# Memory values of three layers from seven block products instead of eight, in five of eight feature pairs

## The chip, the cores and the metric

The kernel runs on one core of one Trainium2 chip. The metric is the device time of one execution in microseconds, the median over the runs of a kernel.

## The reference

A decoder trunk of four layers over 256 tokens of width 2048, all in fp32. Each layer projects its tokens, mixes them in one of three ways, and also lets four memory heads attend to a fixed memory of 256 rows. The part that the change touches is the memory's own projection, which needs no token and is done for all layers before the first layer starts:

```python
mem_n = _rmsnorm(mem, mem_norm)                    # (256, 2048)
for i in range(DEPTH):                             # DEPTH = 4
    ...
    mem_out = _memory_attention(mq, mem_n @ w_mem_kv[i])   # w_mem_kv[i]: (2048, 2048)
# in _memory_attention: mk, mv = jnp.split(mem_kv, 2, axis=-1)   keys: 1024 columns, values: 1024 columns
```

So for every layer a 256 x 2048 matrix is multiplied by a 2048 x 1024 matrix for the keys (mk) and by another for the values (mv).

## The kernel before

fp32 precision is reached with two fp32r parts. Every weight tile `wr` that SyncE loads (128 x 1024, 512 KB) is split: ScalarE copies it to the high part `wh` (line 59, called from `split_in_order`), VectorE subtracts to get the low part `wl` (line 73). The activations are split in the same way once; `mT` holds the memory with features on the partitions, both parts. Each product of a weight tile with an activation tile is then three matmuls of 512 columns: high by high, high by low, low by high (lines 328 to 330 in `rows_by`). There are 5 buffers for `wr` and 3 each for `wh` and `wl`, so the splits run at most a few tiles ahead of TensorE.

`memory()` is the phase of the change. It takes eight turns (i, p_), four layers by two halves of 512 columns. In each turn `rows_by` computes the values' half (accumulator `acc_mv`) and then the keys' half (`acc_mk`), each over 16 feature tiles in steps of two: 96 matmuls, 8 weight tiles. `values` scales the values' accumulator by the row norm, splits it and stores it to DRAM; the keys' accumulator is copied by ScalarE (`mkz`), transposed in blocks by VectorE (`mkT`, line 544) and stored. A table `jobs` puts other work at the sixth feature tile and at the end of a key product: bias tables, loads of x and its first norm (`x_rows`, `x_features`, `nm.chunk`, `nm.finish`), and the eight copies of the bias tables from DRAM to DRAM (`table_copies`, 1.5 MB each, on GpSimd's queue).

The order on every engine comes from a scheduler that follows the program's order and its own estimate of times; splits and the matmuls of the change are pinned to the program's order among themselves. Each engine then runs its queue strictly in that order: an instruction that waits holds up all that stand behind it on that engine. SyncE's queue of loads is such a queue as well.

```python
    def split_in_order(hi, lo, src):
        with ExitStack() as held:
            for ins in behind:
                held.enter_context(tc.issue_after(ins))
            one = copy_act(hi, src)
            two = nc.vector.tensor_sub(lo, src, f32(hi))
        behind[:] = [one.ins, two.ins]
```

Of the kernel before, what the change touches and what calls it, by code (L numbers as in the profile page):

```python
# [8 lines left out]
F32 = mybir.dt.float32  # L9
F32R = mybir.dt.float32r  # L10
# [5 lines left out]
P = 128  # L16
S = 256
# [7 lines left out]
MEMW = 1024  # L25
# [2 lines left out]
PQ, AUX, WR = 5, 4, 5  # L28
IDLE = 9
CAUSAL = [(0, 0), (0, 1), (1, 1)]  # L30


@with_exitstack
def kernel(ctx: ExitStack, tc: tile.TileContext, a: dict, out: bass.AP,
# [20 lines left out]
    def f32(ap):  # L55
        return ap.bitcast(F32)
# [384 lines left out]
    def memory():  # L441
# [44 lines left out]
        def values(i, p_, acc):  # L486
# [6 lines left out]
            for z in range(2):  # L493
                nc.gpsimd.dma_start(mv[i][p_][:, z], v[z])

        def x_features(c):
# [4 lines left out]
        jobs = [[] for _ in range(15)]  # L501
        for at, job in ((0, bias_tables), (0, lambda: x_rows(0)),
                        (1, lambda: x_rows(1)), (2, lambda: x_features(0)), (3, lambda: nm.chunk(0)),
                        (5, lambda: nm.chunk(1)), (6, lambda: x_features(2)), (9, lambda: nm.chunk(2)),
                        (11, lambda: nm.chunk(3)), (12, nm.finish)):
            jobs[at].append(job)
        for n_, at in enumerate((3, 5, 7, 8, 10, 11, 12, 13)):
            jobs[at].append(lambda n_=n_: table_copies(n_ // 4, n_ % 4))
        for i in range(depth):
            w = a["w_mem_kv"][i]  # L510
            for p_ in range(2):
                start = i == p_ == 0
                acc = rows_by(mT, 16, w, 0, (MEMW + p_ * 512, 512), "mv",
                              {s: [lambda s=s: first(s), lambda k, s=s: early(s + k)]
                               for s in range(0, 16, 2)} if start else {},
                              (lambda k, n: loaded(k // 4, k % 4, k % 4 + n) if k else None) if start else None)
                if start:
                    held.append(acc)
                else:
                    values(i, p_, acc)  # L520
                def job():
                    for f in jobs.pop(0):
                        f()
                acc = rows_by(mT, 16, w, 0, (p_ * 512, 512), "mk",
                              {k: [lambda k=k: second(k)] for k in range(0, 14, 2)} if start else {6: [job]})
                T = act.tile([P, 2, 512], F32, name="mkT", tag="pq", bufs=PQ)
                for t in range(2):
                    rows_ = wk.tile([P, 512], F32, name="mkz", tag="z", bufs=2)
                    copy_act(rows_, acc[:, t], scale=m16[:, t:t + 1])
                    turned(T[:, t], rows_, 4)  # L530
# [8 lines left out]
                job()  # L539
        assert not jobs  # L540


    def turned(T, rows_, n):
# [895 lines left out]
```

## Time and profile before

| | us |
|---|---|
| median of 2 runs (2487.89 to 2489.42) | 2488.65 |
| the profiled execution | 2491.03 |
| its span in the profile | 2489.3 |
| TensorE busy | 2474.2 |
| VectorE busy | 1773.7 |
| ScalarE busy | 1401.6 |

The profiled execution is 2.38 us above the median, and 1.73 us of it lie outside the span. Matmuls are pipelined: a matmul of 512 columns is shown with 0.39 us, but the next one starts some 0.23 us after it, so time on TensorE is read from starts. Times inside the profile are counted from the span's start.

### The profile page before, as it was taken

The page shows a single profiled execution, that of the slowest core. Times are in us where ns is not written, and L with a number is a line of the kernel's source. Part 1 is how long each engine was busy: PE and PEld are TensorE (multiplying, and loading weights), DVE is VectorE, ACT ScalarE, POOL GpSimd, SP SyncE. Part 2 cuts the span into 40 slices and gives each one's busy share as a digit, 9 for nine tenths or more (in the row PEclk, how much of TensorE's full clock was granted, in tenths as well). Part 3 has the DMA queues.
Part 4 walks back from the last instruction along what each step waited for, and adds up shares of the span by engine and source line. Part 5 has one row for each costly group of instructions (what it writes and reads, how often), then busy time and mean ns, then how long its engine had stood idle before and what let it go on. Part 6 is the DMA issues. An engine that isn't in the chain of part 4 may idle for free.

```text
span 2489.3 us, 36041 instructions
## 1 busy us (share of the span) xinstructions
PE 2474.2 (99%) x12356; PEld 2084.8 (84%) x12356; DVE 1773.7 (71%) x3025; ACT 1401.6 (56%) x2250; POOL 397.7 (16%) x635
## 2 busy tenths in 40 slices
PE   9999999999999999999999999999999999999998
PEld 7888888888888888887778888878888888888887
DVE  6555655777677676877788776877777677767677
ACT  6444545555555456655566554665665655545554
POOL 1101011211120110012222101212220111012110
PEclk9999999999999999999999999999999999999999
DMA  9888887977877768589999697999978797788874
GB/s 313 279 289 287 285 277 219 259 211 217 220 225 223 220 219 244 190 265 271 258 281 271 201 289 217 288 268 267 271 229 249 231 253 217 199 221 244 242 209 147
DMA packets 462279, 607.57 MB, mean 244 GB/s; under 512 B 79536, under 2 KB 278976, under 8 KB 460944
## 3 DMA queue, kind: packets, MB, share of 16 engines
q1 hardware_dynamic: 420704, 476.92, 64.4%
q0 software_dynamic: 40672, 127.43, 17.2%
q8 instruction: 97, 1.59, 0.3%
q10 hardware_dynamic: 720, 0.93, 0.1%
q14 instruction: 86, 0.70, 0.1%
HBM read 541.49 MB, written 76.25 MB: 248 GB/s over the span
## 4 chain that ended last, share of the span: by engine, by line
PE 96%; DVE 2%; DMA 1%; issue 0%; ACT 0%; SPq 0%; POOL 0%; DVEq 0%; ACTq 0%
PE acc_gr L329 5%; PE acc_gr L328 5%; PE acc_gr L330 5%; PE acc_mq L352 4%; PE acc_g L352 4%; PE acc_wo L328 4%; PE acc_wo L330 4%; PE acc_wo L329 4%; PE acc_qn L352 4%; PE acc_wo L241 3%; PE acc_wo L242 3%; PE acc_wo L243 3%; PE acc_q L329 2%; PE acc_mv L329 2%; PE acc_q L330 2%; PE acc_q L328 2%
## 5 line engine op out<-in xcount | busy, mean ns | idle before, releaser
L73 DVE TENSOR_TENSOR wl<-wr,wh 128x1024 fp32r<-128x1024 f32 (+2 forms) x860 | 1028.2, 1197 | 548.8 <-ACT wh L59 540.2
L59 ACT ACTIVATE wh<-wr 128x1024 fp32r<-128x1024 f32 (+2 forms) x860 | 891.9, 1038 | 814.7 <-PE acc_wo L330 100.6
L329 PE MATMUL acc_gr<-wl,xT 128*128 128x512 f32 x512 | 200.1, 391 | 0.0
L330 PE MATMUL acc_gr<-wh,xT 128*128 128x512 f32 x512 | 199.7, 390 | 0.0
L328 PE MATMUL acc_gr<-wh,xT 128*128 128x512 f32 x512 | 199.7, 390 | 0.0
L328 PE MATMUL acc_wo<-wh,y 128*128 128x512 f32 x432 | 168.5, 390 | 1.9 <-ACT wh L59 1.2
L330 PE MATMUL acc_wo<-wh,y 128*128 128x512 f32 x432 | 168.3, 390 | 0.0
L329 PE MATMUL acc_wo<-wl,y 128*128 128x512 f32 x432 | 168.3, 390 | 0.0
L352 PE MATMUL acc_g<-xT,wh 128*128 128x512 f32 x512 | 161.8, 396 | 0.0
L664 POOL DMA_DIRECT2D pL<-turn x192 | 120.6, 634 | 217.8 <-issue 76.3
L352 PE MATMUL acc_mq<-xT,wh 128*128 128x512 f32 x480 | 151.8, 396 | 0.0
L242 PE MATMUL acc_wo<-wl,y 128*128 128x512 f32 x320 | 124.9, 390 | 0.0
L241 PE MATMUL acc_wo<-wh,y 128*128 128x512 f32 x320 | 124.9, 390 | 0.0
L243 PE MATMUL acc_wo<-wh,y 128*128 128x512 f32 x320 | 124.7, 390 | 0.0
L1336 DVE TENSOR_TENSOR x<-x,acc_wo 128x1024 f32<-128x1024 f32 x92 | 111.5, 1212 | 13.5 <-PE acc_wo L330 9.5
L352 PE MATMUL acc_qn<-cT,wh 128*128 128x512 f32 x384 | 120.5, 396 | 0.0
L354 PEld LDWEIGHTS acc_g<-xT,wl 128*128 128x128 f32 x512 | 95.7, 188 | 22.4 <-DVE z L589 0.8
L329 PEld LDWEIGHTS acc_gr<-wl,xT 128*128 128x128 f32 x512 | 96.1, 188 | 21.1 <-issue 1.9
L328 PEld LDWEIGHTS acc_gr<-wh,xT 128*128 128x128 f32 x512 | 96.2, 188 | 19.4 <-ACT wh L59 0.4
L330 PEld LDWEIGHTS acc_gr<-wh,xT 128*128 128x128 f32 x512 | 96.2, 188 | 19.3
L659 POOL DMA_DIRECT2D turn<-T x56 | 42.9, 766 | 408.0 <-DVE T L653 207.4
L354 PEld LDWEIGHTS acc_mq<-xT,wl 128*128 128x128 f32 x480 | 89.0, 188 | 19.5
(370 smaller groups left out, 5608.4 us busy)
## 6 DMA issues: line engine op xcount, KB each, us to landing
wr<-in_w_out_dram SPq DMA_DIRECT2D x192, 512.0 KB, 4.7
wr<-in_w_in_a_dram SPq DMA_DIRECT2D x176, 512.0 KB, 4.9
wr<-in_w_mem_kv_dram SPq DMA_DIRECT2D x126, 512.0 KB, 6.2
wr<-in_w_in_b_dram SPq DMA_DIRECT2D x116, 512.0 KB, 5.0
wr<-in_w_in_c_dram SPq DMA_DIRECT2D x104, 512.0 KB, 5.3
wr<-in_w_uq_dram SPq DMA_DIRECT2D x192, 128.0 KB, 3.6
turn<-T POOLq DMA_DIRECT2D x40, 384.0 KB, 5.8
tab<-flat POOLq DMA_DIRECT2D x8, 1536.0 KB, 11.8
```

The costliest lines, as they stand in the source:

```text
L59: return nc.scalar.activation(o, i, AF.Copy, scale=scale)
L73: two = nc.vector.tensor_sub(lo, src, f32(hi))
L241: nc.tensor.matmul(accs[c][:, t], xh, wh[:, at], start=first, stop=False)
L242: nc.tensor.matmul(accs[c][:, t], xh, wl[:, at], start=False, stop=False)
L243: nc.tensor.matmul(accs[c][:, t], xl, wh[:, at], start=False, stop=last)
L328: nc.tensor.matmul(acc[:, t, :n], xh, wh[:, at], start=first, stop=False)
L329: nc.tensor.matmul(acc[:, t, :n], xh, wl[:, at], start=False, stop=False)
L330: nc.tensor.matmul(acc[:, t, :n], xl, wh[:, at], start=False, stop=last)
L352: nc.tensor.matmul(acc[j], wh[:, at[j]], q[:, :, kt % 4, :], start=first, stop=False)
L354: nc.tensor.matmul(acc[j][:, 0, :], wl[:, at[j]], q[:, 0, kt % 4, :], start=False, stop=last)
L664: nc.gpsimd.dma_start(f32(self.raw)[j * 32:(j + 1) * 32, :].rearrange("p (i r) -> p i r", r=r), bass.AP(tensor=d.tensor, offset=d.offset + ...
L1336: nc.vector.tensor_add(xs, xs, acc)
```

## The change

The values of layers 1, 2 and 3 no longer come from `rows_by`. A class `Seven` computes all 1024 columns of one layer's values at once, in eight pairs of feature tiles (`BLOCKS = "SSPSPSPS"`). A pair is a product of 2 x 2 blocks: two halves of the memory's rows by two feature tiles, times two feature tiles by two halves of the columns. A block P does the plain eight products (24 matmuls). A block S does seven products (21 matmuls) by Strassen's scheme in Winograd's form, and for that needs four sums of weight blocks and four sums of memory blocks.

- The memory's sums `sT` are made once in the second turn by `row_sums` (per feature chunk one add of 1024 columns, four of 256, and one split of 1024) and kept in buffers that the first layer's norm uses later.
- The weights' sums of an S block are made by `sums`: four subtractions of 512 columns on VectorE, into `w13` and `w24`. Split are then `b11` (512 columns, `wd`), the second weight tile (1024), `w24` (1024) and the two halves of `w13` (512 each): 3584 columns in place of 2048.
- The second weight tile of an S block, `wg`, has no place among the five `wr` buffers; it lies in the place of the gate (`gT`) and of the features (`y`) in turn.
- The seven sums use all eight PSUM banks. After the last block one ScalarE copy and eight VectorE adds of 512 columns put the four quarters of the result together, then `values` runs twice as before.
- `Seven` of layers 1 and 2 runs ahead of the key product of turns (1, 0) and (2, 0), that of layer 3 ahead of turn (2, 1). The sums of its first block are made at the end of the key product before it, and that product's transposes are issued behind them.
- The jobs get four places in each key product (feature tiles 2, 6, 10 and the end). The first norm moves from turns 1 to 6 to turns 5 to 7; the table copies stand at key products alone, two each in those of (1, 0) and (1, 1).

```diff
+            def sums(self, g):
+                wr = [stage(self.w, 2 * g, 1, (MEMW, 1024))[0],
+                      act.tile([P, 2048], F32, name="wg", tag="y", bufs=1)[:, :1024] if self.odd else
+                      act.tile([P, 1024], F32, name="wg", tag="gT", bufs=1)[:]]
...
+                nc.vector.tensor_sub(d1[:, :512], b12, b11)
+                nc.vector.tensor_sub(d2[:, :512], b22, d1[:, :512])
+                nc.vector.tensor_sub(d2[:, 512:], b21, d2[:, :512])
+                last = nc.vector.tensor_sub(d1[:, 512:], b22, b12)
...
+                    if kind == "P":
...
+                                    product(("23", "4p")[t][n], rows_[t][e], z[n])
+                        continue
...
+                    one = self.parts(b11)
+                    z = halves(parts_of(wr, 1024))
+                    product("1", rows_[0][0], one)
+                    product("2", rows_[0][1], z[0])
+                    product("3", s4, z[1])
+                    z = halves(parts_of(d2, 1024))
+                    product("6", s2, z[0])
+                    product("4", rows_[1][1], z[1])
+                    product("5", s1, self.parts(d1[:, :512]))
+                    product("7", s3, self.parts(d1[:, 512:]))
...
+        seven = {(i, 0) if i < 3 else (2, 1): Seven(i) for i in range(1, depth)}
...
+                if (i, p_) in seven:
+                    seven[i, p_].run()
...
+                    with ExitStack() as last:
+                        for ins in ahead:
+                            last.enter_context(tc.issue_after(ins))
+                        turned(T[:, t], rows_, 4)
```

Three places show how the order moves. The first two come again in each of the three changed layers; behind the memory phase, from the first layer on, every queue reads as before.

VectorE's queue before, where the keys of turn (0, 1) end and the values of turn (1, 0) begin; `mkT` waits for the keys' last matmul, `wl` are splits:

```order
L73 TENSOR_TENSOR wl_884<-wr_881,wh_883 128x1024
L73 TENSOR_TENSOR wl_902<-wr_899,wh_901 128x1024
L544 STREAM_TRANSPOSE mkT_866<-mkz_867 128x4x4x32
L544 STREAM_TRANSPOSE mkT_866<-mkz_870 128x4x4x32
L73 TENSOR_TENSOR wl_920<-wr_917,wh_919 128x1024
L73 TENSOR_TENSOR wl_938<-wr_935,wh_937 128x1024
```

The same place now, from the first transpose on; the first S block is split ahead of it, and these rows are the second S block's (`w13_978`, `w24_979`, `wd_985`, `wl_989`) with the sums of the fourth block (`w13_1065`, `w24_1066`) among them:

```order
L529 TENSOR_TENSOR w13_978<-wr_974 128x512
L532 TENSOR_TENSOR w13_978<-wg_976,wr_974 128x512
L665 STREAM_TRANSPOSE mkT_916<-mkz_920 128x4x4x32
L74 TENSOR_TENSOR wd_985<-wr_974,wd_984 128x512
L530 TENSOR_TENSOR w24_979<-wg_976,w13_978 128x512
L74 TENSOR_TENSOR wl_989<-wg_976,wh_988 128x1024
L529 TENSOR_TENSOR w13_1065<-wr_1061 128x512
L531 TENSOR_TENSOR w24_979<-wg_976,w24_979 128x512
L530 TENSOR_TENSOR w24_1066<-wg_1063,w13_1065 128x512
L532 TENSOR_TENSOR w13_1065<-wg_1063,wr_1061 128x512
L531 TENSOR_TENSOR w24_1066<-wg_1063,w24_1066 128x512
L74 TENSOR_TENSOR wl_1002<-w24_979,wh_1001 128x1024
```

Behind the first transpose stand eleven instructions, and only then the low part `wl_1002` that the second block's product 6 needs.

VectorE's queue now, later in the same layer, where the sixth block's low part `wl_1176` stands behind the eighth block's sums (`w13_1239`, `w24_1240`), whose weight tile `wr_1235` takes over the buffer that `wl_1117` read last:

```order
L74 TENSOR_TENSOR wl_1117<-wr_1112,wh_1116 128x1024
L74 TENSOR_TENSOR wl_1133<-wr_1114,wh_1132 128x1024
L74 TENSOR_TENSOR wd_1159<-wr_1148,wd_1158 128x512
L74 TENSOR_TENSOR wl_1163<-wg_1150,wh_1162 128x1024
L529 TENSOR_TENSOR w13_1239<-wr_1235 128x512
L532 TENSOR_TENSOR w13_1239<-wg_1237,wr_1235 128x512
L530 TENSOR_TENSOR w24_1240<-wg_1237,w13_1239 128x512
L531 TENSOR_TENSOR w24_1240<-wg_1237,w24_1240 128x512
L74 TENSOR_TENSOR wl_1176<-w24_1153,wh_1175 128x1024
```

The split is moved behind four subtractions that wait for a load; before, no split stood behind another tile's load.

SyncE's queue now, some 12 us into the kernel; `raw` and `mrow` are the memory, `wr` the first turn's weights, and `wg_908` is a weight tile of turn (1, 0):

```order
L206 DMA wr_284<-in_w_mem_kv_dram 128x2x512
L89 DMA raw_236<-in_c_memT_dram 128x2x256
L525 DMA wg_908<-in_w_mem_kv_dram 128x1024
L206 DMA wr_307<-in_w_mem_kv_dram 128x2x512
L451 DMA mrow_309<-in_mem_dram 128x2x512
L206 DMA wr_332<-in_w_mem_kv_dram 128x2x512
```

Before, the same rows stood there without `wg_908`: it has moved some 80 us ahead of its use, into the start.

## Rows read from the trace of the kernel before

**Rows 1.** The page: the span, and busy time of each engine.

```profile
span 2489.3 us, 36041 instructions
PE 2474.2 (99%) x12356; PEld 2084.8 (84%) x12356; DVE 1773.7 (71%) x3025; ACT 1401.6 (56%) x2250; POOL 397.7 (16%) x635
```

**Rows 2.** Busy time by stretches in the memory phase, one core.

```profile
core 0: us, PE busy (x) PEld busy (x) DVE busy (x) ACT busy (x) POOL busy (x), PEclk, DMA share, GB/s
...
120.00:160.00 40.00, 40.00 (x178) 33.13 (x177) 21.72 (x23) 19.79 (x25) 4.13 (x7) 1.00 0.82 269
160.00:200.00 40.00, 39.90 (x177) 32.69 (x176) 21.77 (x23) 20.14 (x27) 4.12 (x7) 1.00 0.87 296
200.00:240.00 40.00, 40.00 (x178) 33.14 (x177) 21.10 (x19) 17.74 (x19) 4.69 (x8) 1.00 0.85 289
```

**Rows 3.** All that TensorE waited for from 0 to 430 us.

```profile
engine line waited for: us in total, times, longest us
PE idle L106 <- DVE warm L108: 1.1, 1, 1.1
PE acc_mv L329 <- DVE wl L73: 0.7, 3, 0.2
PE acc_mv L328 <- ACT wh L59: 0.5, 1, 0.5
```

**Rows 4.** Timeline of a key product: start, duration, engine, what, idle time ahead.

```profile
128.37 1.06 ACT L59 ACTIVATE wh<-wr 128x1024 fp32r<-128x1024 f32 x1 [1.66 <-PE acc_mk L330]
...
129.47 1.23 DVE L73 TENSOR_TENSOR wl<-wr,wh 128x1024 fp32r<-128x1024 f32 x1 [1.49 <-ACT wh L59]
...
131.09 1.06 ACT L59 ACTIVATE wh<-wr 128x1024 fp32r<-128x1024 f32 x1 [1.66 <-PE acc_mk L330]
```

**Rows 5.** Groups of VectorE's instructions by form: count, busy us, mean ns.

```profile
L73 DVE TENSOR_TENSOR wl<-wr,wh 128x1024 fp32r<-128x1024 f32 x812 | 992.0, 1223 | 516.2 <-ACT wh L59 507.9 <-DMA wr<-in_w_uq_dram 1.9 <-PE isp L1107 1.3
...
L491 DVE SCALAR_TENSOR_TENSOR mv<-acc_mv,mrstd,mv 128x512 fp32r<-128x512 f32 x16 | 12.0, 748 | 8.3 <-ACT mv L59 8.3
...
L826 DVE TENSOR_TENSOR qrr<-qrr,rot 128x256 f32<-128x256 f32 x16 | 6.7, 418 | 0.1
...
L73 DVE TENSOR_TENSOR wl<-wr,wh 128x512 fp32r<-128x512 f32 x8 | 5.4, 691 | 2.7 <-ACT wh L59 2.5
...
L1234 DVE TENSOR_TENSOR x<-x,acc_wo 128x512 f32<-128x512 f32 x7 | 4.6, 680 | 0.8 <-PE acc_wo L1243 0.8
```

**Rows 6.** Timeline where a key product ends, ScalarE and VectorE.

```profile
51.23 1.27 ACT L59 ACTIVATE mkz<-acc_mk,m 128x512 f32<-128x512 f32 x2 [1.61 <-PE acc_mk L330]
...
51.95 1.31 DVE L544 STREAM_TRANSPOSE mkT<-mkz 128x512 f32<-128x512 f32 x2 [1.08 <-ACT mkz L59]
```

**Rows 7.** DMA issues of the whole page: KB each, median us to landing.

```profile
wr<-in_w_out_dram SPq DMA_DIRECT2D x192, 512.0 KB, 4.7
...
tab<-flat POOLq DMA_DIRECT2D x8, 1536.0 KB, 11.8
```

**Rows 8.** Landing times of the weight tiles between 60 and 420 us.

```profile
DMA to landing us min/median/max: 2.8/5.2/13.4
```

**Rows 9.** DMA issues between 60 and 100 us.

```profile
wr<-in_w_mem_kv_dram SPq DMA_DIRECT2D x14, 512.0 KB, 7.1
```

**Rows 10.** Timeline of the start: a split that waited for its load, and its use.

```profile
26.60 1.06 ACT L59 ACTIVATE wh<-wr 128x1024 fp32r<-128x1024 f32 x1 [1.75 <-DMA wr<-in_w_mem_kv_dram]
...
27.69 1.22 DVE L73 TENSOR_TENSOR wl<-wr,wh 128x1024 fp32r<-128x1024 f32 x1 [3.14 <-ACT wh L59]
...
29.27 0.39 PE L328 MATMUL acc_mk<-wh,mT 128*128 128x512 f32 x1
29.50 0.39 PE L329 MATMUL acc_mk<-wl,mT 128*128 128x512 f32 x1
```

**Rows 11.** Busy time by stretches at the start; columns as in rows 2.

```profile
25.00:30.00 5.00, 5.00 (x24) 4.14 (x23) 1.22 (x1) 3.25 (x6) 0.00 (x0) 1.00 1.04 385
```

More of the change, by code (lines that the diff above doesn't have):

```diff
@@ L494, in values, with row_sums @@
                 nc.gpsimd.dma_start(mv[i][p_][:, z], v[z])
+        sT = []
+        def row_sums(c):
+            a_ = act.tile([P, 1024], F32, name="rowsA", tag="pq", bufs=PQ)[:].rearrange(
+                "p (g e t b) -> p g e t b", g=2, e=2, t=2)
+            z = act.tile([P, 1024], F32, name="rowsS", tag="pq", bufs=PQ)
+            nc.vector.tensor_add(a_.rearrange("p g e t b -> p (g e t b)"),
+                                 f32(mT[c])[:, 0].rearrange("p k s -> p (k s)"),
+                                 f32(mT[c])[:, 1].rearrange("p k s -> p (k s)"))
+            a11, a12, a21, a22 = (a_[:, :, e, t] for t in range(2) for e in range(2))
+            s_ = z[:].rearrange("p (n g b) -> p n g b", n=4, g=2)
+            nc.vector.tensor_add(s_[:, 0], a21, a22)
+            nc.vector.tensor_sub(s_[:, 1], s_[:, 0], a11)
+            nc.vector.tensor_sub(s_[:, 2], a11, a21)
+            nc.vector.tensor_sub(s_[:, 3], a12, s_[:, 1])
+            q = act.tile([P, 2, 1024], F32R, name="sT", tag="xT", bufs=4)
+            split(q[:, 0], q[:, 1], z)
+            sT.append(q[:].rearrange("p v (n g b) -> p v n g b", n=4, g=2))
@@ L500, in memory @@
         held = []
[L501 to L505, printed above, removed]
+        jobs = [[] for _ in range(8 * depth)]
+        for at, job in ((3, bias_tables), (3, lambda: x_rows(0)), (5, lambda: x_rows(1)),
+                        (4, lambda: row_sums(0)), (4, lambda: row_sums(1)),
+                        (5, lambda: row_sums(2)), (6, lambda: row_sums(3)),
+                        (20, lambda: x_features(0)), (22, lambda: nm.chunk(0)), (24, lambda: nm.chunk(1)),
+                        (25, lambda: x_features(2)), (26, lambda: nm.chunk(2)), (28, lambda: nm.chunk(3)),
+                        (29, nm.finish)):
             jobs[at].append(job)
[L507 removed]
+        for n_, at in enumerate((9, 10, 13, 14, 17, 21, 27, 30)):
             jobs[at].append(lambda n_=n_: table_copies(n_ // 4, n_ % 4))
[L509 removed]
+        seven = {(i, 0) if i < 3 else (2, 1): Seven(i) for i in range(1, depth)}
+        turns = [(i, p_) for i in range(depth) for p_ in range(2)]
+        for i, p_ in turns:
             w = a["w_mem_kv"][i]
[L511 removed]
+            if True:
                 start = i == p_ == 0
[L513 removed]
+                n_ = turns.index((i, p_))
+                if (i, p_) in seven:
+                    seven[i, p_].run()
+                ahead = []
+                acc = None if i else rows_by(mT, 16, w, 0, (MEMW + p_ * 512, 512), "mv",
                               {s: [lambda s=s: first(s), lambda k, s=s: early(s + k)]
@@ L518, in memory, with job, first_sums @@
                     held.append(acc)
-                else:
+                elif i == 0:
                     values(i, p_, acc)
-                def job():
-                    for f in jobs.pop(0):
-                        f()
-                acc = rows_by(mT, 16, w, 0, (p_ * 512, 512), "mk",
-                              {k: [lambda k=k: second(k)] for k in range(0, 14, 2)} if start else {6: [job]})
+                def job(at):
+                    for f in jobs[4 * n_ + at]:
+                        f()
+                    jobs[4 * n_ + at] = []
+                def first_sums():
+                    if n_ + 1 < len(turns) and turns[n_ + 1] in seven:
+                        ahead.append(seven[turns[n_ + 1]].sums(0))
+                hooks = {k: [lambda k=k: second(k)] for k in range(0, 14, 2)} if start else {
+                    s: [lambda at=at: job(at)] for at, s in enumerate((2, 6, 10))}
+                hooks[14] = [first_sums]
+                acc = rows_by(mT, 16, w, 0, (p_ * 512, 512), "mk", hooks)
                 T = act.tile([P, 2, 512], F32, name="mkT", tag="pq", bufs=PQ)
@@ L538, in memory @@
                     late_constants()
-                job()
-        assert not jobs
+                job(3)
+        assert not any(jobs)
     def turned(T, rows_, n):
```

56 lines of the change are left out of this document (55 added, 1 removed).

## The prediction

> **What bounds the kernel now.** I read the page first: TensorE is busy 99% of the span [rows 1]. Then the stretches of the memory phase: TensorE full, granted clock 1.00 throughout, VectorE busy 21 to 22 of 40 us, ScalarE 18 to 20 [rows 2]. Then TensorE's own waits: in the first 430 us, 1.2 us for splits and 1.1 us at the very start [rows 3]. The timeline shows why: ScalarE sits idle 1.66 us until a matmul frees a `wh` buffer, VectorE waits for ScalarE, and the pattern repeats every 131.09 - 128.37 = 2.72 us, one step of 12 matmuls [rows 4]. So the phase is bound by TensorE, at 2.72 / 12 = 0.2267 us a matmul, and the splits run ahead. The question is whether they still do.
>
> **What is removed.** A layer's values took 192 matmuls. Five blocks of 21 and three of 24 are 177. Three layers save 45 x 0.2267 = 10.2 us. Nothing else leaves the path.
>
> **VectorE's load in a changed layer.** An S block has four subtractions of 512 columns, splits of three times 512 and of twice 1024. From both forms of line 73, 691 and 1223 ns [rows 5], that is 7 x 0.69 + 2 x 1.22 = 7.3 us, against 21 x 0.2267 = 4.76 us on TensorE. A P block has 2.4 against 5.44. A layer (first sums made ahead) comes to 5 x 7.3 - 2.8 + 3 x 2.4 = 40.9 us at full durations, against 177 x 0.2267 = 40.1 us. Before, the same stretch had some 22 of 40. Back to back the instructions overlap a little: two transposes of 692 ns take 1.31 us [rows 6], 0.65 each. I step with 0.65 for 512 columns and 1.17 for 1024, which gives 37.9 us. VectorE is thus as loaded as TensorE, its order decides, and whatever idles it is felt. ScalarE, with 3.5 us an S block, is not the limit.
>
> **The second S block.** Let 0 be the moment when ScalarE starts on the finished keys. TensorE began the first S block just before, at -0.2, with its splits made ahead. VectorE gets its first transpose 0.72 us after ScalarE's start [rows 6]. The second order shown in the section on the change then has that transpose and eleven instructions, eleven of 512 columns and one of 1024, ahead of `wl_1002`: 0.72 + 11 x 0.65 + 1.17 = 9.0, and `wl_1002` ends at 10.3. TensorE wants it for the 32nd matmul of the layer: -0.2 + 31 x 0.2267 = 6.8. It waits 3.5 us. With 0.63 in place of 0.65 it is 3.2, with full durations 3.9; this happens in every changed layer, as the transposes of a key product stand there each time. Three times 3.5 is 10.5 us: the saving is gone already.
>
> **The waits for loads.** In the later S blocks the next one's sums stand ahead of the split of `w24`, and wait for a tile whose buffer was freed only 1.17 + 0.65 + 1.17 = 3.0 us of VectorE's work earlier (third order shown). With a landing time of L, VectorE idles L + 0.1 - 3.0. L here is 2.8 at least, 5.2 in the median [rows 8], 7.1 beside x's loads [rows 9], 4.7 for tiles of the same size elsewhere [rows 7]. I take 4.7, since in these stretches no table copy starts: 1.8 us idle, twice. Stepping on: behind `wl_1002` come six splits (3 x 0.65 + 3 x 1.17 = 5.5), the idle time and three sums, so `wl_1089` of the fourth block ends at 10.3 + 5.5 + 1.8 + 3 x 0.65 + 1.2 = 20.75; TensorE wants it after the second block's remaining 11 matmuls (12.8), a P block (18.25) and ten matmuls, at 20.5: 0.25 late. then four instructions of 512 columns and three of 1024 (6.1), the idle time and four sums, and `wl_1176` of the sixth ends at 20.75 + 6.1 + 1.8 + 2.6 + 1.2 = 32.45, wanted at 20.75 + 2.5 + 5.44 + 2.27 = 30.95: 1.5 late. The eighth block has no sums behind it and is in time. That is 1.75 us a layer, 5.25 in all; with L = 2.8 nothing, with 5.2 2.7 a layer, with 7.1 6.5.
>
> On this the Trainium skill has a rule: the page DMA: Bandwidth & Descriptors (Anatomy of one DMA, a fit for GpSimd's queue) puts a transfer at about 2.0 us plus its bytes over 436 GB/s, an estimate of 3.2 us for 512 KB. By it this term would be nearly nothing and the sum about 5 us lower; the trace's median of 5.2 speaks against it, its least, 2.8, for it, and I keep to the rows.
>
> **The smaller terms.** (a) The key product behind `Seven` needs a PSUM buffer whose bank 6 is read by the first of the eight adds, which stands behind two splits: 0 to 0.7 us (one add, 680 ns [rows 5]) each time, I take 0.5, 1.5 in all. (b) The other adds (0.68 us each) and the four scaled splits (0.748) bring VectorE's load in that key product to 8 x 1.22 + 2 x 0.69 + 5.4 + 3.0 = 19.6 of 21.8 us, under cover of TensorE; where the next layer's first sums come on top it is 22.4, and the lead of the splits covers it; cost 0 to 1, taken as 0. (c) The row sums: per chunk 1.22 + 4 x 0.42 + 1.22 = 4.1 us, 16.5 us in a turn of 43.5 us, where VectorE has some 20 us idle [rows 2]. They fit, with 2.8 us of first sums nearly to the brim: 0 to 2, I take 0.6. (d) `wg_908` stands in the start's queue. There the DMA moves 385 GB/s [rows 11] and a split waited 1.75 us for its load; the low part ended at 28.91 and was used at 29.50 [rows 10]. 512 KB are 1.4 us more, less the margin of 0.6: 0.8 us late. (e) Four table copies of 11.8 us [rows 7] now fall within two key products of 43.5 us in sum, beside 8.4 MB of weights; weights 8.4, copies 6.3, stores 3 MB are 17.7 MB, 407 GB/s, more than the 385 of rows 11. The five buffers give several steps of slack and the copies can run on into layer 2's values, where they lengthen L: 0 to 4 us, I take 1. (f) The first norm's work moves to turns with a key product alone, 21.8 us with 11 us of VectorE's work; no cost, and its result is needed only by the layers.
>
> **Sum.** -10.2 + 10.5 + 5.25 + 1.5 + 0.6 + 0.8 + 1.0 = +9.45 us, on 2491.03 of the profiled execution: 2500.5. That execution lies 2.4 above the median, so 2498 for the median of runs.
>
> **Rivals.** *The saving shows.* If VectorE keeps its lead over the key product's end better than I stepped (the transposes' wait then costs about 1 us a layer) and loads land in 3 us, what is left is 3 x 1 + 1.5 + 0.8 us, and the time is 2488.65 - 10.2 + 5.3 = 2484. For it: VectorE's sum of work, 37.9 us, is below TensorE's 40.1. Against: the transposes and the next sums stand in its queue in an order that no margin covers. *Late loads.* With L = 7.1 the waits for loads are 6.5 us a layer, 19.5 in place of 5.25: 2512. For it: rows 9, and the table copies of (e); against: the median of 5.2, and that the tile waited for is the first of its burst. *The clock falls.* The waits leave TensorE idle for some microseconds in one place, and its clock is granted by its activity; if it fell to 1.2 GHz for the changed layers, their 531 matmuls would take up to twice their 120 us: 2498 + 120 = 2618, and from about a third of that stretch at the lower level the kernel is more than 2% slower. Against: the clock was 1.00 in each stretch [rows 2, 11], the start's waits included, and no wait that I step through is longer than 3.5 us. The Trainium skill's page TensorE: Matmul & The Clock Gate (Part 1) says that the throttled state is the default and that activity releases it; no run here shows it at work.
>
> **How the numbers follow.** The forecast gets 0.58, its own range 2490 to 2506 (first wait 3.2 to 3.9, L 4 to 5.5); the saving that shows 0.20, at 2478 to 2489; late loads 0.20, 2506 to 2520; the clock 0.02. The range 2484 to 2513 holds the forecast and somewhat more than half of the two rivals beside it. 2% is 50 us, about what a measurement of this kernel can tell from no change. Faster by that is out of reach, since the whole saving is 10 us: 0.01. Slower by that needs the clock: 0.02. Within 2%: 0.97.
>
> **What would show it.** Right: in the changed profile TensorE has 45 matmuls less; in each of three stretches of some 46 us it waits first for about 3.5 us on a `wl` or `wh` in the second block, then for 1 to 2 us in the sixth, named after VectorE; VectorE is busy some 85% there, and its idle time ahead of line 529 is put down to the weights' DMA. The first step is wrong if TensorE waits under 2 us at the second block; the second if line 529 never waits for a DMA; the whole if these stretches take 41 us or less.

## The result, and the profile after

The changed kernel takes 2513.96 us (median of 2 runs, 2512.01 to 2515.91) against 2488.65 us: a ratio of 1.0102, interval 1.0058 to 1.0145. It is 25.3 us slower; the forecast was 2498.0, and the time lies 0.96 us above the upper end of the range. The profiled execution took 2515.91 us at a span of 2514.1.

The page after, as [rows 1] of before: 45 matmuls fewer, VectorE 87 us busier.

```profile
span 2514.1 us, 36138 instructions
PE 2479.5 (99%) x12311; PEld 2082.0 (83%) x12311; DVE 1860.5 (74%) x3178; ACT 1429.9 (57%) x2302; POOL 397.6 (16%) x635
```

TensorE is still 99% busy, and yet 5.3 us busier than before with fewer matmuls; some of them ran at a lower clock, as shown below. Where the time went is read from the first matmul of layer 0, in TensorE's timeline of before and of after (start, duration, engine, line, tile):

```profile
357.55 0.39 PE L259 MATMUL acc_cq<-wh,xT 128*128 128x512 f32 x1
```

```profile
384.07 0.39 PE L260 MATMUL acc_cq<-wh,xT 128*128 128x512 f32 x1
```

It starts 26.5 us later, and from there to the end the kernel takes 2130.0 us (2514.1 - 384.07) against 2131.75. In this execution all of the loss is in the memory phase. TensorE's longest waits there, as [rows 3]:

```profile
PE acc_st L553 <- DVE wl L74: 6.5, 3, 3.7
PE acc_mk L329 <- ACT wh L60: 6.1, 3, 4.6
PE acc_st L553 <- ACT wh L60: 5.5, 3, 4.2
PE acc_mk L330 <- DVE wl L74: 2.0, 3, 0.8
PE idle L107 <- DVE warm L109: 1.1, 1, 1.1
PE st L553 <- DVE wl L74: 0.9, 2, 0.5
PE acc_mk L329 <- DVE u L587: 0.7, 3, 0.2
```

`acc_st` and `st` are the banks of the new values, `acc_mk` a key product. So there are two kinds of wait: in the values, as forecast, and in key products, whose code did not change. The stretches of 40 us that answer to [rows 2]:

```profile
120.00:160.00 40.00, 39.76 (x175) 32.38 (x174) 31.68 (x38) 21.72 (x27) 3.26 (x6) 1.00 0.67 230
160.00:200.00 40.00, 31.92 (x122) 24.39 (x121) 16.52 (x18) 13.53 (x16) 3.57 (x6) 0.91 0.93 329
200.00:240.00 40.00, 38.03 (x163) 29.99 (x162) 35.80 (x47) 22.61 (x29) 2.49 (x4) 1.00 0.61 203
```

The middle one, 160 to 200 us, lies in the key products of layer 1: TensorE has 122 matmul records where it had 177, VectorE and ScalarE idle most of the time, and the DMA engines are 93% busy at 329 GB/s. DMA issues between 140 and 200 us (tile, queue, count, KB each, median us to landing):

```profile
wr<-in_w_mem_kv_dram SPq DMA_DIRECT2D x17, 512.0 KB, 5.9
tab<-flat POOLq DMA_DIRECT2D x4, 1536.0 KB, 15.2
```

Four table copies of 1.5 MB take 15.2 us each in the median, where all eight took 11.8 before [rows 7]. They are issued in pairs 0.5 us apart, at 155.66 and 156.19 and again at 170.21 and 170.75 us. The median of 17 loads hides the worst of them. From 156 to 181 us the DMA engines are busy all the time (share 1.02) at 353 GB/s, and the seven weight tiles issued there land after 13.2 to 24.6 us. A key product lasts 21.8. ScalarE waits for such a tile, and TensorE for ScalarE:

```profile
156.00:181.00 25.00, 22.04 (x94) 17.13 (x93) 9.56 (x9) 7.51 (x8) 4.29 (x8) 1.00 1.02 353
wr<-in_w_mem_kv_dram SPq DMA_DIRECT2D x7, 512.0 KB, 18.2
186.65 1.06 ACT L60 ACTIVATE wh<-wr 128x1024 fp32r<-128x1024 f32 x1 [7.64 <-DMA wr<-in_w_mem_kv_dram]
187.76 0.79 PE L329 MATMUL acc_mk<-wh,mT 128*128 128x512 f32 x1 [4.64 <-ACT wh L60]
```

The third layer's values have long waits too. TensorE's timeline there; in brackets the idle time before and what ended it:

```profile
277.06 0.80 PE L553 MATMUL acc_st<-wh,sT 128*128 128x512 f32 x1 [4.18 <-ACT wh L60]
281.61 0.80 PE L553 MATMUL acc_st<-wl,sT 128*128 128x512 f32 x1 [3.75 <-DVE wl L74]
```

and VectorE's, a little ahead of them:

```profile
274.55 0.69 DVE L529 TENSOR_TENSOR w<-wr 128x512 f32<-128x512 f32 x1 [3.14 <-DMA wr<-in_w_mem_kv_dram]
278.52 0.69 DVE L530 TENSOR_TENSOR w<-wg,w 128x512 f32<-128x512 f32 x1 [2.68 <-DMA wg<-in_w_mem_kv_dram]
```

These subtractions belong to the fourth block, and wait for its weights; the splits of the second block stand behind them in VectorE's queue, and TensorE waits for those. The loads were issued at 259 to 263 us, just behind the single copy of turn (2, 0) at 258.83, and landed after 13.6 to 15.7 us. That is the forecast's chain, with loads later than it assumed. In layer 1's values VectorE waits once in the second block, too, for 0.65 us:

```profile
103.49 0.69 DVE L530 TENSOR_TENSOR w<-wg,w 128x512 f32<-128x512 f32 x1 [0.65 <-DMA wg<-in_w_mem_kv_dram]
```

No table copy is in flight there, since the first one is issued at 155.66.

Stretches around the waits show what comes on top. The eighth column is the granted clock:

```profile
100.00:107.00 7.00, 4.04 (x15) 2.58 (x14) 6.35 (x9) 4.04 (x6) 2.11 (x4) 0.92 0.83 282
107.00:113.00 6.00, 6.00 (x16) 4.63 (x16) 5.00 (x7) 1.52 (x2) 0.00 (x0) 0.53 0.44 137
113.00:143.00 30.00, 30.00 (x132) 24.32 (x130) 23.08 (x28) 17.05 (x21) 0.00 (x0) 1.00 0.57 196
188.00:194.00 6.00, 5.53 (x13) 3.96 (x14) 4.03 (x5) 2.74 (x3) 0.00 (x0) 0.50 0.72 279
276.00:282.00 6.00, 1.19 (x2) 0.68 (x3) 3.48 (x5) 4.46 (x6) 0.00 (x0) 0.54 0.46 166
282.00:288.00 6.00, 6.00 (x18) 4.73 (x18) 5.18 (x7) 1.06 (x1) 0.00 (x0) 0.61 0.39 124
288.00:318.00 30.00, 29.76 (x131) 24.07 (x129) 23.34 (x29) 17.04 (x21) 0.00 (x0) 1.00 0.60 202
```

In the 6 us behind the waits at 104 to 107 us TensorE is busy all the time and does 16 matmuls in place of 26: the granted clock is 0.53, close to the lower level of 1.2 GHz, and then 1.00 (2.4 GHz) again. The same comes behind the waits in the key products of layer 1 and in layer 3's values. The Trainium skill's page TensorE: Matmul & The Clock Gate (Part 1) has the throttled state as the default, which activity releases; here rows agree. Matmuls at the lower level start 0.43 us apart (190.04, 190.47) in place of 0.2267. Added up over the starts, the lower clock costs 3.0 us in layer 1's values, 2.7 in the key products of layer 1 and 2.5 in layer 3's values, 8.2 us in all.

Where the 26.5 us are, stretch by stretch (lengths from first matmul to first matmul of the next group; the matmuls alone are 177 x 0.2267 = 40.1 us for a layer's values, 43.5 for the key products of layer 1):

- values of layers 1, 2, 3: 47.47, 44.07, 52.30 us, that is 7.35 + 3.95 + 12.18 = 23.5 over the matmuls;
- key products of layer 1: 56.33, 12.8 over;
- the start 0.3, the other key products 0.5; a wait of 0.4 that before had is gone;
- 45 matmuls: -10.2.

Of the 36.3 us in the first two lines, 25.7 are waits (from start to start), 8.2 the lower clock, and 2.4 small delays.

### The profile page after: what moved, and what is told of

Its sections match the earlier page's. It is cut to its first block, busy times and chain, and to the rows that moved or that the text cites. A ratio compares the mean times of both kernels' runs of the same rounds, so it can differ in the third digit from the quotient of the medians.

```text
span 2514.1 us, 36138 instructions
## 1 busy us (share of the span) xinstructions
PE 2479.5 (99%) x12311; PEld 2082.0 (83%) x12311; DVE 1860.5 (74%) x3178; ACT 1429.9 (57%) x2302; POOL 397.6 (16%) x635
## 4 chain that ended last, share of the span: by engine, by line
PE 89%; DVE 5%; DMA 4%; issue 1%; ACT 1%; SPq 0%; ACTq 0%; DVEq 0%
PE acc_mq L353 4%; PE acc_g L353 4%; PE acc_gr L330 4%; PE acc_gr L329 4%; PE acc_gr L331 4%; PE acc_wo L329 4%; PE acc_wo L331 4%; PE acc_wo L330 4%; PE acc_qn L353 4%; PE st L553 3%; PE acc_wo L243 3%; PE acc_wo L242 3%; PE acc_wo L244 3%; PE acc_q L330 2%; PE acc_q L331 2%; PE acc_q L329 2%
## 5 line engine op out<-in xcount | busy, mean ns | idle before, releaser
L74 DVE TENSOR_TENSOR wl<-wr,wh 128x1024 fp32r<-128x1024 f32 (+2 forms) x830 | 991.0, 1196 | 474.6 <-ACT wh L60 465.9
L60 ACT ACTIVATE wh<-wr 128x1024 fp32r<-128x1024 f32 (+2 forms) x830 | 859.6, 1037 | 762.7 <-PE acc_wo L331 96.9
L329 PE MATMUL acc_mk<-wh,mT 128*128 128x512 f32 x256 | 101.5, 397 | 6.8 <-ACT wh L60 6.1
```

The costliest lines, as they stand in the source:

```text
L60: return nc.scalar.activation(o, i, AF.Copy, scale=scale)
L329: nc.tensor.matmul(acc[:, t, :n], xh, wh[:, at], start=first, stop=False)
```

## Experiments

Theory 1: the table copies, which the new job table sets more densely, delay the memory's weight loads. Theory 2: VectorE's order (transposes and the next block's sums ahead of splits) makes it late. Theory 3: the amount of VectorE's work in a layer's values does. The runs came in four groups, each with runs of the kernel before on the same chip beside it. All of them compute everything; "copies" are the eight table copies. Lengths are from each run's profiled execution, in us:

| run | median | before | ratio (interval) | values of layers 1, 2, 3 | keys of layer 1 | last three key products | layer 0 starts |
|---|---|---|---|---|---|---|---|
| before | 2488.65 | | | 43.5 (192 matmuls) | 43.5 | 65.8 | 357.55 |
| changed | 2513.96 | 2488.65 | 1.0102 (1.0058 to 1.0145) | 47.47, 44.07, 52.30 | 56.33 | 66.14 | 384.07 |
| g_plain | 2504.21 | 2490.74 | 1.0049 (1.0032 to 1.0067) | 43.52, 44.48, 43.52 | 53.17 | 66.02 | 369.81 |
| a_copies | 2507.82 | 2490.74 | 1.0059 (1.0039 to 1.0080) | 44.17, 45.62, 44.06 | 48.89 | 74.27 | 374.66 |
| b_order | 2512.06 | 2490.74 | 1.0079 (1.0061 to 1.0098) | 45.68, 43.74, 45.74 | 56.30 | 66.68 | 376.11 |
| c_copies_order | 2505.83 | 2490.74 | 1.0060 (1.0040 to 1.0080) | 45.66, 46.03, 45.78 | 43.66 | 72.62 | 371.71 |
| h_plain_out | 2493.74 | 2490.01 | 1.0016 (1.0007 to 1.0025) | 43.52, 43.52, 43.52 | 43.52 | 65.76 | 357.31 |
| i_seven_out | 2494.46 | 2490.01 | 1.0017 (1.0008 to 1.0027) | 43.96, 44.03, 44.08 | 43.66 | 65.90 | 359.38 |
| j_order_late_out | 2496.15 | 2490.01 | 1.0027 (1.0016 to 1.0039) | 44.55, 44.55, 44.88 | 43.65 | 65.89 | 360.82 |
| l_pool_out | 2516.19 | 2490.01 | 1.0106 (1.0091 to 1.0121) | 53.19, 50.54, 52.40 | 43.66 | 65.90 | 383.71 |
| o_pfirst | 2495.78 | 2490.20 | 1.0018 (1.0010 to 1.0027) | 42.50, 41.59, 44.14 | 48.64 | 65.89 | 360.75 |
| p_sfirst | 2496.26 | 2490.20 | 1.0022 (1.0013 to 1.0031) | 42.04, 42.18, 42.98 | 49.73 | 65.76 | 360.47 |
| q_five | 2506.69 | 2490.20 | 1.0063 (1.0049 to 1.0077) | 46.81, 45.63, 47.23 | 50.42 | 65.91 | 373.91 |
| r_three | 2504.28 | 2490.20 | 1.0052 (1.0039 to 1.0065) | 43.41, 43.93, 47.86 | 49.07 | 65.89 | 368.32 |
| s_four_out | 2487.07 | 2490.57 | 0.9984 (0.9976 to 0.9993) | 42.52, 41.59, 41.59 | 44.50 | 65.89 | 353.49 |
| t_four_order_out | 2487.21 | 2490.57 | 0.9984 (0.9975 to 0.9992) | 42.60, 41.64, 41.64 | 43.65 | 65.91 | 353.24 |
| u_three_out | 2495.15 | 2490.57 | 1.0014 (1.0005 to 1.0022) | 44.16, 44.46, 43.64 | 43.66 | 65.90 | 359.83 |
| v_before_out | 2491.24 | 2490.57 | 1.0000 (0.9991 to 1.0008) | as before | as before | 65.8 | 356.92 |

**First group: the parts of the change apart.** g_plain keeps the new order of the phase and its jobs, without S blocks and without sums:

```diff
-BLOCKS = "SSPSPSPS"
+BLOCKS = "PPPPPPPP"
```

> The changed kernel with all eight blocks plain (24 matmuls each): no sums of weights or memory, no combining adds, 45 matmuls more; job table, copies and the order of turns as changed. Theory 1 (copies): the two key products behind layer 1's values still lose about 12 us, the three layers' values lose nothing: 2489 + 12 = 2501 us. Theory 2 (VectorE's load and order make all of the loss): no stall is left, 2489 us.

12.3 us are lost with no S block at all: 9.65 in the key products of layer 1, 1.5 in the next, 1 in the values of layer 2. Its loads between 140 and 200 us:

```profile
wr<-in_w_mem_kv_dram SPq DMA_DIRECT2D x18, 512.0 KB, 14.2
tab<-flat POOLq DMA_DIRECT2D x4, 1536.0 KB, 16.5
```

A weight tile lands after 14.2 us in the median. GpSimd issues the copies and SyncE the loads; the Trainium skill's page DMA: Bandwidth & Descriptors (Issuing engines are not separate DMA queues) says that both run on the same 16 engines and interleave, and these rows agree.

a_copies spreads the copies (four at other key products, four in layer 0):

```diff
-        for n_, at in enumerate((9, 10, 13, 14, 17, 21, 27, 30)):
+        for n_, at in enumerate((9, 13, 22, 26)):
...
+            if i == 0 and part < 4:
+                table_copies(1, part)
```

> The changed kernel with one edit: of the eight table copies, the first four stand one each at four key products, (1, 0), (1, 1), (2, 1) and (3, 0), and the last four in layer 0, one at each of its first four token parts. Theory 1 (the crowded copies hold back the weight loads): the two key products behind layer 1's values lose at most 1 us in place of 12.8, layer 3's values lose about 5 in place of 12.2, so about 2514 - 19 = 2495 us. Theory 2 (the order in VectorE's queue is what costs, whatever the loads do): layer 1's and 3's values still lose 7 to 12 us, only the key products gain, about 2502 or more.

b_order issues the four subtractions behind the splits of the block before:

```diff
+                    for ins in behind:
+                        held.enter_context(tc.issue_after(ins))
```

> The changed kernel with one edit: the four sums of a block are issued behind the splits of the block before it, so that no split stands behind another block's load. Copies as changed. Theory 1 (copies): the key products still lose 12 us and layer 3's loads are still late, at most 6 us gained, 2508 or more. Theory 2 (order): every changed layer gains 3 to 8 us, about 2514 - 15 = 2499 us, and TensorE's wait in the second block falls below 1 us.

c_copies_order has both edits:

> Both edits, spread copies and sums behind the splits. If both theories hold each for its part: 2514 - 19 - 9 = 2486 us, with TensorE's clock 1.00 in the whole memory phase; if only the copies count, 2495; if only the order counts, 2499.

The copies move the loss with them, but one at a time they still cost. In a_copies the keys of layer 1 lose 5.4 us in place of 12.8, and the last key products, which now have two single copies early in them, lose 8.5 in place of 0.4. The time is 2507.82 us, not theory 1's 2495. The order alone (b_order) leaves the key products at 56.3, as theory 1 said, but layer 3's values fall from 52.30 to 45.74 with the copy of turn (2, 0) still ahead of them: the loads beside it land after 9.6 to 11.3 us, and the splits no longer stand behind them. With both edits the time is 2505.83, not 2486. The keys of layer 1 lose nothing, though the copies there are those of a_copies; why, the third group shows. The last key products still lose 6.8, with no S block behind them. In c_copies_order ScalarE waits there for x's load, beside a copy, and the next weight tiles' splits stand behind that instruction:

```profile
337.56 1.71 ACT L60 ACTIVATE xT<-raw,gvec 128x256 fp32r<-128x256 f32 x4 [7.16 <-DMA raw<-in_c_xT_dram]
341.49 0.50 PE L329 MATMUL acc_mk<-wh,mT 128*128 128x512 f32 x1 [4.03 <-ACT wh L60]
```

In all three runs the values still take 43.7 to 46.0 us, over the 43.5 of 192 plain matmuls.

**Second group: the copies out of the memory phase** (four in layer 0, four in layer 1).

```diff
-        for n_, at in enumerate((9, 10, 13, 14, 17, 21, 27, 30)):
-            jobs[at].append(lambda n_=n_: table_copies(n_ // 4, n_ % 4))
...
+            if i < 2 and part < 4:
+                table_copies(i, part)
```

h_plain_out is g_plain with this edit:

> All eight blocks plain (24 matmuls each, no sums of weights or rows), so 45 matmuls more than the changed kernel and as many as before; the eight table copies stand in layers 0 and 1, none in the memory phase. Theory 1 (crowded table copies): the 12 us that the plain version lost with the changed places of the copies go away; layer 0's first product starts near 357.6 us as before (within 2), the two key products of layer 1 take 43.5 to 44.5 us in place of 53.2, and the time is 2489 to 2492. Rival (it is the new order of the jobs, or one layer's values over eight banks, that costs): key products still 48 us or more, 2498 or more.

i_seven_out is the changed kernel with this edit alone:

> The changed kernel with the table copies alone moved to layers 0 and 1. Theory 1: the two key products of layer 1 come back to 43.5 to 44.5 us (changed: 56.3), and the values of layer 3 lose their two waits of 4.3 us. Theory 2 (VectorE's order) then shows alone: each of the three stretches of values takes 44.5 to 46 us, where the matmuls alone take 40.1, as in the run with spread copies and sums behind the splits (45.7 to 46.0); time 2494 to 2500. If the copies were behind the waits in the stretches of values too, these take 41 to 43 us and the time is 2482 to 2488.

Theory 1 holds for the key products and for layer 3's values. In h the phase is as long as before, every stretch at its matmuls; the new job table costs nothing of its own there. (Its time, 2493.74, is 1.7 us over what was expected.) In i the key products come back from 56.33 to 43.66, layer 3's values from 52.30 to 44.08. The time falls from 25.3 us over before to 4.5 (1.8 of it in the memory phase).

Layer 1's values come back too, from 47.47 to 43.96, but this isn't the copies' doing: up to 142 us TensorE, VectorE, ScalarE and SyncE have the same instructions in the same order in both runs, and no copy has been issued. The runs differ there by VectorE's wait of 0.65 us for `wg`, shown above, after which TensorE waited 2.01 us in place of 1.27 and its clock fell. q_five and a_copies have the same instructions up to there as well: q_five takes 46.81 us, with a wait of 1.23 for `wg` and the lower clock behind it, a_copies 44.17. So a load that lands less than a microsecond later went with some 3 us of difference, most of it by the clock.

TensorE's longest waits from 0 to 400 us in i:

```profile
PE acc_st L553 <- DVE wl L74: 2.9, 3, 1.3
PE st L553 <- DVE wl L74: 2.2, 2, 1.1
PE acc_st L553 <- ACT wh L60: 1.6, 3, 0.9
PE idle L107 <- DVE warm L109: 1.1, 1, 1.1
PE acc_mk L329 <- DVE u L587: 0.7, 3, 0.2
```

What is left are the splits of the S blocks. The values take 44.0 us: S blocks save 3.4 us a layer and lose 3.9. The clock stays at 1.00; the longest wait is 1.3 us.

j_order_late_out adds two edits of order: the sums behind the splits as in b_order, and the keys' two transposes behind the third block.

```diff
+                    if g == LATE:
+                        later()
```

> Table copies in layers 0 and 1; the sums of an S block issued behind the splits of the one before; the two transposes of the keys ahead of a changed layer issued behind its third block instead of in the middle of its second. Theory 2: the waits in the second block (0.3 to 1.2 us each) fall to under 1 us a layer, the clock stays at 1.00, and the stretches of values take 41 to 43 us: 2484 to 2489. Rival 3 (VectorE has no room at all: its 38 to 41 us of work in 40.1 us of matmuls keep it late whatever the order): 45 us or more each, 2496 or more.

The values take 44.6 to 44.9 us, no less than i's and just short of rival 3's 45: those two places of the order are not what makes five blocks late. VectorE is busy 44.95 us of the 50 from 95 to 145 us.

l_pool_out gives the subtractions to GpSimd:

```diff
-                nc.vector.tensor_sub(d1[:, :512], b12, b11)
+                nc.gpsimd.tensor_sub(d1[:, :512], b12, b11)
```

> Table copies in layers 0 and 1; the four subtractions of each S block on GpSimd in place of VectorE, all else as changed. VectorE's work per S block falls by 4 x 0.69 = 2.8 us, to some 4.5 against 4.76 us of matmuls. How long GpSimd takes for 512 columns no run has shown: from 0.69 (VectorE's) to four times that, 2.8 us, so 2.8 to 11 us a block; an S and a P block last 10.2 us. Theory 2 and rival 3 alike (VectorE's work is what is late): stretches of values of 41 to 43 us, 2483 to 2489. If GpSimd's four take more than about 8 us, or slow VectorE down beside them, the sums are late and the stretches take 45 us or more, 2496 or more.

This missed the 41 to 43 us on the slow side, with 50.5 to 53.2. Two of GpSimd's groups (count, busy us, mean ns):

```profile
L532 POOL TENSOR_TENSOR w<-wg,wr 128x512 f32<-128x512 f32 x15 | 28.6, 1910 | 2.2 <-DMA wg<-in_w_mem_kv_dram 2.2
L531 POOL TENSOR_TENSOR w<-wg,w 128x512 f32<-128x512 f32 x15 | 25.7, 1714 | 0.9
```

and VectorE's splits of 512 columns beside them, in l and then in i, both from 95 to 145 us:

```profile
L74 DVE TENSOR_TENSOR wd<-w,wd 128x512 fp32r<-128x512 f32 x10 | 14.1, 1451 | 0.0
```

```profile
L74 DVE TENSOR_TENSOR wd<-w,wd 128x512 fp32r<-128x512 f32 x10 | 6.5, 682 | 0.0
```

All four lines together take 6.9 us a block, and VectorE's 512-column splits of the sums double. So this run doesn't tell what VectorE would gain by less work. The Trainium skill's page GPSIMD Engine Reference (4.1 Engine selection) has GpSimd about twice as slow at such operations; here the four lines take 1.5 to 1.9 us on average against 0.68, two to three times as long, and the measurement decides.

**Third group: fewer S blocks**, with three copies left at key products (of turns (1, 0), (1, 1), (2, 0)) and five in layer 0.

```diff
-BLOCKS = "SSPSPSPS"
+BLOCKS = "PSPSPSPS"
```

> Four S blocks a layer in place of five, in the order P S P S P S P S; copies: three at the key products of (1, 0), (1, 1) and (2, 0), five in layer 0. 36 matmuls are saved, 8.2 us; a layer's values are 180 matmuls, 40.8 us, and VectorE's work is 4 x 7.3 + 4 x 2.4 - 2.8 = 36.0 us, with two transposes 37.4. Theory 3 (VectorE's amount of work made the five-block stretches late): no wait over 0.5 us, stretches of 41 to 41.7 us, 2482 to 2486. Theory 2 (what counts is that an S block comes first, with the transposes and the next sums ahead of its successor): the same here, since a P block comes first, but not in the run with S first. If both fall: 43 us or more, 2490 or more.

> As the run with four S blocks, in the order S P S P S P S P. The same matmuls and the same work for VectorE. Theory 3: stretches of 41 to 41.7 us, 2482 to 2486, as with P first. Theory 2: the transposes and the next block's sums stand ahead of the first splits that follow, waits of 1 to 2 us a layer in the first three blocks, 42.5 to 43.5 us, 2487 to 2491.

> The changed kernel (five S blocks, its own order) with the copies as in the runs with four S blocks. Stretches of values of 43.9 to 44.2 us, as with the copies in layers 0 and 1; layer 0's first product starts 1.5 to 2.5 us later than before; no loss in the layers, so 2490 to 2493. If the copies at three key products disturb the values behind them, stretches of 45 us or more and 2495 or more.

> Three S blocks a layer, P S P P S P P S, the same copies. 27 matmuls are saved, 6.1 us; VectorE's work is 3 x 7.3 + 5 x 2.4 - 2.8 = 31.1 us in 183 x 0.2267 = 41.5. Theory 3: stretches of 41.5 to 42, 2484 to 2487, some 1 to 2 us above four blocks, since nothing is left to gain by less work for VectorE. If VectorE was still late with four, this is as fast as four or faster.

(p_sfirst has "SPSPSPSP", q_five the changed kernel's own blocks, r_three "PSPPSPPS".) In layers 1 and 2 the values of four blocks take 41.6 to 42.5 us, P first or S first: near the expected gain, and Theory 2 has nothing to show in that. In layer 3, beside the third copy, they take 44.14 and 42.98. The times of o_pfirst, p_sfirst and r_three lie above those that the theories gave; of q_five the second case came true (45 us or more, 2495 or more). The four runs lose 5 to 7 us in the keys of layer 1, where two single copies are in flight, and q_five is 12 us in all slower than i. VectorE and TensorE in o_pfirst, at the end of those keys:

```profile
177.14 0.69 DVE L529 TENSOR_TENSOR w<-wr 128x512 f32<-128x512 f32 x1 [5.98 <-DMA wr<-in_w_mem_kv_dram]
177.75 0.68 DVE L532 TENSOR_TENSOR w<-wg,wr 128x512 f32<-128x512 f32 x1
178.35 0.68 DVE L530 TENSOR_TENSOR w<-wg,w 128x512 f32<-128x512 f32 x1
178.96 1.22 DVE L74 TENSOR_TENSOR wl<-wr,wh 128x1024 fp32r<-128x1024 f32 x1
180.23 0.50 PE L330 MATMUL acc_mk<-wl,mT 128*128 128x512 f32 x1 [3.04 <-DVE wl L74]
```

The first sums of layer 2's values wait 5.98 us for a weight tile, and the keys' own split stands behind them. That is why c_copies_order, whose sums are issued behind splits, lost nothing in these keys with the same copies, and a_copies, which differs by this order alone, lost 5.4. One copy a key product did harm where something that waits for a load stood ahead of the keys' splits: sums here, x's features in the last key products of the first group. Four copies in two pairs did harm without that (g_plain). Whether it is the pairing or the number of copies isn't separated: every run with single copies also has fewer of them in these two key products.

**Fourth group: fewer blocks with all copies behind the phase** (one at each of the six parts of layer 0, two in layer 1).

```diff
+            if i * 6 + at < 8:
+                table_copies(*divmod(i * 6 + at, 4))
```

> Four S blocks a layer (P S P S P S P S), all eight table copies behind the memory phase: one at each of the six places of layer 0, two in layer 1. Theory 3 (the amount of VectorE's work; five blocks lost 3.9 us a layer without copies) with theory 4 (a copy beside the memory's weights delays the load that the sums in VectorE's queue wait for, which cost 5 us in the key products of layer 1 and 3 us in layer 3's values in the two runs with four blocks): every stretch of values 41.2 to 42 us, key products of layer 1 43.5 to 44 us, layer 0's first product at 353 to 355.5; 2486 to 2490. If waits of over 2 us stay where no copy is in flight, theory 4 falls.

> The same, with the sums of an S block issued behind the splits of the block before. Theory 4: with no copies in flight there is no late load to step out of the way of, so nothing is won against the run without this order: within 1 us of it in the memory phase. Theory 2: another 0.5 to 1 us a layer is won.

> Three S blocks a layer (P S P P S P P S), all copies behind the memory phase. 183 matmuls a layer, 41.5 us. Theory 3: VectorE has 10 us to spare, the stretches take 41.5 to 42 us, the memory phase is as long as with four blocks or 1 us longer. If four were still short of VectorE's time, it is shorter than with four.

> The kernel before, with nothing changed but that its eight table copies stand in layers 0 and 1 in place of the memory phase. It shows what that place costs by itself: the all-plain version with copies in these layers was 3.7 us slower than before though its memory phase took as long. If the place costs it, this is 2 to 4 us slower than before; if the layers only scatter from run to run, it is within 1 us.

s_four_out is faster than both kernels, if by far less than 2%: 2487.07 us against 2490.57 of before in the same group, ratio 0.9984 (0.9976 to 0.9993). Layer 0 starts 4.1 us sooner than before, and of TensorE's waits in the values one of 0.6 us is left (layer 1's 42.52 and its keys' 44.50 are 0.5 us more than expected):

```profile
PE acc_mk L329 <- DVE u L587: 0.7, 3, 0.2
PE st L553 <- DVE wl L74: 0.6, 1, 0.6
PE acc_mk L330 <- DVE wl L74: 0.6, 1, 0.6
```

The order (t_four_order_out) changes the phase by 0.25 us: with loads in time it does not matter, as expected. v_before_out shows that this place of the copies costs or gives before nothing beyond the interval (2 us to either side). u_three_out missed: three blocks take 43.6 to 44.5 us, more than four. VectorE around its fifth and sixth block in layer 1:

```profile
119.95 0.69 DVE L529 TENSOR_TENSOR w<-wr 128x512 f32<-128x512 f32 x1 [1.87 <-DMA wr<-in_w_mem_kv_dram]
...
122.97 1.22 DVE L74 TENSOR_TENSOR wl<-wr,wh 128x1024 fp32r<-128x1024 f32 x1
```

TensorE then waits 0.69 us for that `wl`, at 124.24. The subtraction is of the eighth block's sums. VectorE had room (37 of 50 us busy) and spent it waiting for a load, with the sixth block's split behind. The same comes twice in each of layers 2 and 3 (TensorE waits 0.3 to 0.7 us, some 4.3 us behind VectorE's wait). So Theory 3 in its plain form falls: VectorE's work alone doesn't set the loss; at which block sums wait for a load counts as well. How the 3.9 us that five blocks lose without copies divide between the two isn't shown.

## Why the prediction was wrong

**The step that failed is (e), the table copies**: 0 to 4 us, taken as 1. It measured 20.9 us. With the copies gone (i_seven_out) the keys of layer 1 came back by 12.7 us and layer 3's values by 8.2; by the medians it is 20.8 (25.3 over before against 4.5). Three things were wrong in it.

- It set the 407 GB/s that are wanted against the 385 that the DMA engines moved at the start, and called the five buffers slack for the rest. With copies in flight the engines were fully busy at 353 GB/s. By that rate its own 17.7 MB take 50.1 us in place of 43.5, an estimate from these two numbers.
- The copies were issued in pairs, and weight tiles issued beside them landed after 13.2 to 24.6 us. Five buffers at one tile in 2.72 us reach 13.6 us.
- It looked at the copies of layer 1 alone. That of turn (2, 0) ran on into layer 3's values, and the loads that its sums wait for landed after 13.6 to 15.7 us where L = 4.7 was taken, "since in these stretches no table copy starts".

**A second term was put at nothing: the clock.** It cost 8.2 us. Some 5.2 of them are within the 20.9, behind the copies' waits; 3.0 are in layer 1's values, where no copy is in flight. The rival was held off because "no wait that I step through is longer than 3.5 us", but in layer 1 the clock fell behind two waits of 0.95 and 2.01. It was also priced for whole layers (120 us), while it fell for some 7 to 10 us at a time.

The other terms, against the run without copies, i_seven_out:

- *45 matmuls, -10.2*: right; 12356 became 12311.
- *Second S block, 3.5 us a layer*: right in place and order. From start to start it is 3.4 in layer 1 and 2.1 in layer 2 of the changed kernel, and 2.65 to 2.8 a layer without copies (in layer 1 the brackets show 0.95 and 1.27; a wait delays the start by 0.16 us more). The `wl` stepped through ended 9.7 us behind ScalarE's start on the keys, where 10.3 was predicted.
- *Waits for loads, 1.75 a layer*: VectorE did idle ahead of line 529 for the weights' DMA, 0.9 to 1.0 us for the sixth and eighth block's sums of layer 1 in i_seven_out, but TensorE did not wait there; near 0 without copies. With (a), 0.42 a layer (0.5 predicted), and what is left of small gaps, the values lose 11.7 us where 17.25 were predicted.
- *VectorE's load*: the steps of 0.65 and 1.17 add up to 38.9 us, not 37.9, and with the two transposes to 40.2, against TensorE's 40.1. The number entered no term of the sum, but it was the case for *the saving shows*.
- *Row sums*: 0 (turn 2 took 44.50 us before and after); *`wg_908` at the start*: 0.3 in place of 0.8.

So without the copies the forecast's sum would have been +8.45, and the memory phase measured +1.8: the terms of the S blocks were half as large again as measured, that of the copies some twenty times too small. The first error hid 5.5 us of the second, and it is by luck that the time came out only 0.96 us outside the range. Of the rivals, *late loads* (2512) came nearest and named the copies, but made them an L of 7.1 us in the values, while half the loss was in plain key products. *The saving shows* (2484) is near what four blocks and late copies give.

Open: the medians of h_plain_out, i_seven_out, j_order_late_out and u_three_out are 2 to 4 us slower than their memory phases explain, those of s_four_out, t_four_order_out and v_before_out by about 1. Each memory phase was read from one execution, and from layer 0's first matmul to the end the profiled executions last 2128.0 (u) to 2140.1 us (h), before 2131.7; where in the layers that lies wasn't traced. Open too are pairing against number of the copies, and why the last key products of a_copies wait for x's load when before, with single copies beside x's loads, does not.

## What to carry to other kernels

A background transfer is priced at the rate that the DMA engines reach while it is in flight, and by what else is issued beside it, not by a rate seen elsewhere; when a job table is made anew, every DMA in it is looked up again, also those that have nothing to do with the edit. An instruction that waits for a load and stands ahead of splits in an in-order queue hands its wait to everything behind it, so operations on raw weights are placed where nothing urgent is queued behind. Waits of a few microseconds on TensorE can cost some 3 us more by its clock. Trading matmuls for VectorE's work pays only while that engine has room in the same stretch: five blocks of eight gave back more than they saved, four, with loads in time, kept half of it.

## What was not expected of the hardware

- The granted clock of a kernel that is 99% busy falls at single places: 0.53 from 107 to 113 us, 0.50 from 188 to 194 and 0.54 to 0.61 from 276 to 288, right behind waits that add up to 3.0, 5.1 and 7.9 us. The sum of the waits doesn't tell by itself whether it falls. In b_order it was 0.50 from 107 to 110 us behind waits of 1.07 and 0.76; in o_pfirst a single wait of 2.27 at 264 us left it at 1.00, and so did 2.0 us in four waits in layer 2's values of the changed kernel.
- One 1.5 MB copy within DRAM at a time landed in 10 to 15 us in the memory phase. Weight tiles issued just behind it landed after 6.5 to 11.8 us in the key products of layer 1 in c_copies_order; beside two pairs of copies in the changed kernel they took 13.2 to 24.6.
- A subtraction of 512 columns took GpSimd 1.5 to 1.9 us, and VectorE's splits of the 512-column sums beside it took 1.45 in place of 0.68.
